# A diffusion-transformer kernel: the last output tile's second half in column parts of 384 and 128, in place of 256 and 256

## The chip, the cores and the metric

One NeuronCore of one Trainium2 chip runs the whole kernel. The metric is the device time of one execution in microseconds. The kernel before took 1170.2 us, the median of three runs that lie between 1170.05 and 1171.52 us. One further execution was recorded by the profiler; every trace number below comes from it.

## What is computed

The reference is a two-layer network on 256 latent tokens and 256 context tokens of width 1024. Each layer has adaptive modulation, a token mixer (retention in the first layer, neighbourhood attention in the second), a gated residual with layer norm, and a squared-ReLU MLP with hidden width 4096. Only the last lines of the second layer matter here:

```python
def sq_relu_mlp(h, w1, w2):
    return jnp.square(jax.nn.relu(h @ w1)) @ w2

x = layer_norm(DN_ALPHA * x + g1 * y, ln_g[i, 0], ln_b[i, 0])
h = x * (1.0 + sc2) + sh2
x = layer_norm(DN_ALPHA * x + g2 * sq_relu_mlp(h, mlp_w1[i], mlp_w2[i]), ln_g[i, 1], ln_b[i, 1])
```

In the last layer only the 256 latent rows go through the MLP, and the last `layer_norm` writes the output.

## The kernel before

Every product of two float32 matrices is made as three products of rounded operands. Each operand is split into a high part in the type float32r and a low part (the value less its high part, again float32r), and `mm3` issues high*high, high*low and low*high into one PSUM accumulator. Each of the three is its own MATMUL with its own weight load (LDWEIGHTS).

The second matrix of the last MLP (4096 x 1024) is streamed from memory in 32 **units** of 256 rows x 512 columns: SyncE issues the load into `raw` (a ring of four buffers), ScalarE makes the high part (`hi`, a CAST), VectorE makes the low part (`lo`). The high and low tiles come from rings of five (`hip`, `lop`); three more homes in freed memory (`spares`) hold units fetched further ahead, and these are called `unit` in the trace. `fetch_ahead` decides which unit goes where.

The hidden activations `hid` are stationary: each weight load brings 128 hidden channels x 128 tokens into the array, and the unit's columns stream past it. The output has two token tiles (t = 0, 1) of 128 rows, and two halves of 512 columns each. Four accumulations, each in PSUM banks of its own, are kept open over the whole of the MLP:

- (0,0), (0,1) and (1,0) each have one bank and one part of 512 columns;
- (1,1), the last tile's second half, has two banks. `parts[1, 1]` lists the columns of each.

The loop `for step in range(24)` takes one unit at a time (u = step // 2, half = step % 2) and calls `mm2b(t, half, u, un)` for both tiles. `mm2b` runs over the parts of that accumulation, and for each part issues 2 x 3 = 6 MATMULs. So the split of (1,1) is used in **every** odd step, not at the end alone: in each of the 12 odd steps part 0 gets six MATMULs and then part 1 gets six.

The last eight units are held (`held`), and the tail uses them accumulation by accumulation, so that the accumulations end one after the other: (0,0), (0,1), (1,0), then part 0 of (1,1) in 24 MATMULs, then part 1 of (1,1) in 24 MATMULs. Behind each, VectorE multiplies the product by the gate `G2`, adds it to the residual `R`, and takes the row statistics (`bn_stats`). For the second token tile this goes by four pieces, called quarters: `gate_quarter`, `add_quarter` and `stat_quarter` for q = 0 to 3. `moments` joins the four statistics, GpSimd makes the reciprocal standard deviation, and `finish_last` makes the two passes of the layer norm and starts the last three stores (512, 256 and 256 columns).

The order of the instructions on each engine is written by hand from the tail on (`e.on = True`). Before that, in the 24 steps, PE, ScalarE, VectorE and GpSimd are ordered by the scheduler of the tile framework, which works from its own estimate of times; SyncE is always in program order, apart from where that estimate places an instruction.

Of the kernel before, what the change touches and what calls it, by code (L numbers as in the profile page):

```python
# [93 lines left out]
def kernel(  # L94
# [23 lines left out]
    pe, act, dve, pool, sp = (  # L118
        InOrder(tc, getattr(nc, e), e in PIN)
        for e in ("tensor", "scalar", "vector", "gpsimd", "sync")  # L120
    )
# [19 lines left out]
    def nm(s):  # L141
        uid[0] += 1
        return f"{s}_{uid[0]}"

    def bank(s="ps"):
        return psp.tile([P, 512], F32, tag="ps", name=nm(s))
# [5 lines left out]
    def scr(s, dt=F32):  # L152
        return scp.tile([P, 512], dt, tag="scr", name=nm(s))
# [201 lines left out]
    R = [RR[t // 2][:, t % 2, :] for t in range(4)]  # L355
# [232 lines left out]
    def load_gate(l, w, nt=2, eng=nc.scalar):  # L588
        G = cpool.tile([P, 2, D], F32, tag="G", name=nm("G"))
        gt = grow[l, w]  # L590
        for t in range(nt):
            eng.dma_start(out=G[:, t, :], in_=gt[t : t + 1, :].broadcast_to([P, D]))
        return G
# [486 lines left out]
    for h in range(RH):  # L1080
# [105 lines left out]
        for t in range(4):  # L1186
            po = bank("po")
            scs = list(range(4)) if t < 2 else [2, 3]
            for i, sc in enumerate(scs):
# [9 lines left out]
                out=on, in0=po[:], scalar1=mv[:, 0:1], scalar2=r[:], op0=ALU.subtract, op1=ALU.mult  # L1199
# [47 lines left out]
        else:  # L1247
# [17 lines left out]
            def turn(t):  # L1265
                return [mod_pt(xns[t], half) for half in range(2)]
# [75 lines left out]
    G2 = None  # L1342
    for hf in range(2):
# [9 lines left out]
        if hf == 0:  # L1353
# [6 lines left out]
            p2 = turn(2)  # L1360
# [45 lines left out]
        for half in range(2):  # L1406
# [14 lines left out]
            for u in range(8 - nheld):  # L1421
# [4 lines left out]
                if G2 is None and bg_done[0] >= 36:  # L1426
                    G2 = load_gate(0, 1)
# [21 lines left out]
            def settle(t):  # L1449

                add_to(t, 1, gated(pb[t], t, 1, G2), dve)
                stat(t, 1)
                return moments(t)
# [13 lines left out]
            m = settle(0)  # L1467
# [5 lines left out]
            m = settle(1)  # L1473
# [9 lines left out]
            m = settle(2)  # L1483
# [328 lines left out]
    m = settle(3)  # L1812
# [3 lines left out]
    p2 = turn(2)  # L1816
# [144 lines left out]
    def wo_last(ps, t, half, cols=slice(0, 512), first=False):  # L1961
        mmo(ps, t, (4, 5, 6, 7), us[half::2], cols, first)
        return ps
# [13 lines left out]
    ps = wo_last(bank("pnw"), 0, 0, first=True)  # L1977
# [61 lines left out]
    ps = [bank("pnw") for _ in range(2)]  # L2039
# [63 lines left out]

    FULL = slice(0, 512)
    parts = {(t, half): [(bank("p2"), FULL)] for t, half in ((0, 0), (0, 1), (1, 0))}
    parts[1, 1] = [(bank("p2"), slice(256 * q, 256 * q + 256)) for q in range(2)]

    def mm2b(t, half, u, un, only=None):
        wh, wl = un
# [32 lines left out]
    for step in range(24):  # L2142
# [7 lines left out]
        if step == 11:  # L2150
            bg_until(83)
            G2 = load_gate(1, 1, 1)
# [6 lines left out]
        e.on = True  # L2159
    st1 = scr("st1")[:, :24].rearrange("p (q s) -> p q s", q=4)  # L2160

    def quarter(q):
        return slice(256 * q, 256 * q + 256)

    gq = {}

    def gate_quarter(q):
        ps = parts[1, q // 2][(q // 2) * (q % 2)][0][:, quarter(q % 2)]
        gq[q] = scr("acc")
        dve.tensor_mul(out=gq[q][:, :256], in0=ps, in1=G2[:, 0, quarter(q)])  # L2170

    def add_quarter(q):
        dve.tensor_add(out=R[1][:, quarter(q)], in0=R[1][:, quarter(q)], in1=gq[q][:, :256])

    def stat_quarter(q):
        dve.bn_stats(out=st1[:, q, :], in_=R[1][:, quarter(q)])
# [3 lines left out]
    def store(t, sl, q=sp):  # L2180
        q.dma_start(out=by_grid(out[0], t)[:, :, sl], in_=xn2[:, t, sl])

    def last_norm(t, a, sl, mv, r, q=sp):

        xn = xn2[:, t, sl]
        dve.scalar_tensor_tensor(
            out=xn,
            in0=xn if a else R[t][:, sl],
            scalar=r[:] if a else mv[:, 0:1],
            in1=gb[:, a, sl],  # L2190
            op0=ALU.mult if a else ALU.subtract,
            op1=ALU.add if a else ALU.mult,
        )
        if a:
            store(t, sl, q)
# [8 lines left out]
    def finish_last(m):  # L2204
        for half in range(2):
            last_norm(1, 0, HALF[half], *m)
        last_norm(1, 1, HALF[0], *m)
        for q, queue in ((2, act), (3, sp)):
            last_norm(1, 1, quarter(q), *m, queue)

    for half in range(2):
        for u in range(12, 16):
# [10 lines left out]
    for q in range(4):  # L2223
        gate_quarter(q)
        add_quarter(q)
        stat_quarter(q)
    stats[1] = st1
    finish_last(moments(1))


# [29 lines left out]
```

## Time and profile before

| what | before |
|---|---|
| median of the runs | 1170.2 us |
| lowest and highest run | 1170.05, 1171.52 us |
| the profiled execution, whole time | 1170.31 us |
| its span, first to last instruction | 1168.4 us |
| granted TensorE clock, mean | 0.998 |
| DVE, ACT, POOL busy | 67%, 45%, 14% of the span |
| first matmul of the last product | 1071.30 us |
| last matmul of it begins | 1159.96 us |
| VectorE's last instruction begins | 1164.42 us, 0.48 us long |

All trace times are microseconds from the span's start; the profiled execution is 1.9 us longer than its span. In the views, PE is the matmul side of TensorE and PEld its weight loads, DVE is VectorE, ACT is ScalarE, POOL is GpSimd, SP is SyncE, and a q behind a name is the engine's own queue. A row of the timeline gives start, length, engine, line, operation, output<-inputs, the tile of the array in rows*columns (for PE), the operand's shape, and xN where N instructions alike were merged into one row, from the first start to the last end. Almost all rows have line 84, which is the helper that records every operation, so tiles are told apart by their names: `p` is a product in PSUM, `hi`, `lo` and `unit` are weights, `hid` the hidden activations. In the PE rows the type of float32r operands is printed as f32.

In the trace matmuls overlap: those of 256 columns are printed as 0.28 us long and start 0.12 us apart. What a stream of matmuls costs is read from the distance between starts.

### The profile page before, as it was taken

What the parts mean: (1) busy time and instruction counts of PE and PEld (TensorE: products, weight loads), DVE (VectorE), ACT (ScalarE), POOL (GpSimd) and SP (SyncE); (2) the same over time, 40 slices, a digit from 0 to 9 for tenths busy, and PEclk for the clock granted to TensorE, in tenths of its full rate; (3) what the DMA queues carried; (4) which work ended last, traced back from release to release, by engine and by line L of the source; (5) the groups of instructions that cost most, each with busy time, mean ns of one, the idle gap of its engine ahead of it and who ended that gap; (6) DMA issues with size and microseconds to landing.
All of it is one profiled execution on the core that took longest, in us unless ns stands there. A gap on an engine that the chain in (4) does not pass through costs nothing.

```text
span 1168.4 us, 18111 instructions
## 1 busy us (share of the span) xinstructions
PE 1154.2 (99%) x7114; PEld 977.5 (84%) x7114; DVE 779.5 (67%) x1223; ACT 520.6 (45%) x900; POOL 157.9 (14%) x187
## 2 busy tenths in 40 slices
PE   9999999999999999999999999999999999999997
PEld 6788888888888889888888788889777879999886
DVE  3585797689597476368877666658456578865555
ACT  3643342243323247442123553127466685776350
POOL 0102002100200150000202000221253450000000
PEclk9999999999999999999999999999999999999999
DMA  9742552856345224357665667635634453686860
GB/s 322 236 130 87 162 166 78 297 154 213 98 148 185 78 59 120 87 146 247 203 198 166 213 200 249 201 108 184 200 112 154 143 187 109 203 252 225 272 221 36
DMA packets 134470, 200.06 MB, mean 171 GB/s; under 512 B 16193, under 2 KB 76385, under 8 KB 134385
## 3 DMA queue, kind: packets, MB, share of 16 engines
q1 hardware_dynamic: 129696, 185.69, 50.2%
q0 software_dynamic: 3296, 10.55, 2.9%
q10 hardware_dynamic: 1392, 2.67, 0.7%
q8 instruction: 56, 0.92, 0.3%
q14 instruction: 30, 0.24, 0.1%
HBM read 190.36 MB, written 10.61 MB: 172 GB/s over the span
## 4 chain that ended last, share of the span: by engine, by line
PE 82%; DVE 6%; DMA 6%; ACT 3%; issue 2%; POOL 1%; DVEq 0%; POOLq 0%; ACTq 0%; SPq 0%
PE p L84 34%; PE pw L84 7%; PE pv L84 7%; PE pq L84 7%; PE pg L84 7%; PE pnv L84 4%; PE pn L84 3%; PE po L84 3%; DVE acc L84 2%; DMA rawa<-in_ada_w_dram 2%; PE pnw L84 2%; DMA raw<-in_mlp_w_dram 2%; PE pS L84 1%; DVE lo L84 1%; PE pt L84 1%
## 5 line engine op out<-in xcount | busy, mean ns | idle before, releaser
L84 ACT CAST hi<-raw 128x1024 fp32r<-128x1024 f32 (+1 forms) x222 | 222.4, 1012 | 323.5 <-DMA raw<-in_mlp_w_dram 115.4
L84 DVE TENSOR_TENSOR lo<-raw,hi 128x1024 fp32r<-128x1024 f32 (+1 forms) x210 | 249.6, 1200 | 131.5 <-ACT hi L84 129.5
L84 PE MATMUL p<-hi,hid 128*128 128x512 f32 (+1 forms) x792 | 230.7, 373 | 0.0
L84 PE MATMUL p<-hTh,hi 128*128 128x256 f32 (+1 forms) x512 | 168.5, 330 | 0.0
L84 PE MATMUL p<-hTh,lo 128*128 128x256 f32 (+1 forms) x512 | 168.0, 329 | 0.0
L84 PEld LDWEIGHTS p<-hi,hid 128*128 128x128 f32 x792 | 145.0, 188 | 26.0
L84 PE MATMUL p<-hTl,hi 128*128 128x256 f32 (+1 forms) x512 | 166.2, 329 | 0.0
L84 PE MATMUL p<-lo,hid 128*128 128x512 f32 (+1 forms) x396 | 147.4, 372 | 0.0
L84 PEld LDWEIGHTS p<-hTh,lo 128*128 128x128 f32 x512 | 97.3, 190 | 8.8
L84 PEld LDWEIGHTS p<-hTh,hi 128*128 128x128 f32 x512 | 97.3, 190 | 8.7
L84 PEld LDWEIGHTS p<-hTl,hi 128*128 128x128 f32 x512 | 96.3, 190 | 8.6
L84 DVE SCALAR_TENSOR_TENSOR acc<-rawa,scol,acc 128x1024 f32<-128x1024 f32 x63 | 80.8, 1309 | 21.5 <-DMA rawa<-in_ada_w_dram 21.2
L84 PEld LDWEIGHTS p<-lo,hid 128*128 128x128 f32 x396 | 74.6, 188 | 12.8
L84 DVE SCALAR_TENSOR_TENSOR strips<-rawa,scol,strips 128x512 f32<-128x512 f32 x84 | 57.5, 744 | 0.0
L84 DVE TENSOR_TENSOR hid<-r,hid 128x512 fp32r<-128x512 f32 (+1 forms) x60 | 33.5, 571 | 30.6 <-ACT hid L84 30.6
L84 ACT ACTIVATE r<-p 128x512 f32<-128x512 f32 (+1 forms) x60 | 29.7, 496 | 52.2 <-PE p L84 52.1
L84 POOL DMA_DIRECT2D grow<-grow x6 | 3.3, 557 | 366.5 <-DVE grow L84 366.5
L84 PE MATMUL pw<-hi,oh 128*128 128x512 f32 x128 | 50.8, 397 | 0.0
L84 PE MATMUL pg<-hi,hTh 128*128 128x512 f32 x128 | 50.6, 396 | 0.0
L84 PE MATMUL pv<-hi,hTh 128*128 128x512 f32 x128 | 50.4, 394 | 0.0
L84 PE MATMUL pw<-hi,ol 128*128 128x512 f32 x128 | 49.9, 390 | 0.0
L84 PE MATMUL pg<-hi,hTl 128*128 128x512 f32 x128 | 49.9, 390 | 0.0
(235 smaller groups left out, 2251.9 us busy)
## 6 DMA issues: line engine op xcount, KB each, us to landing
raw<-in_mlp_w_dram SPq DMA_DIRECT2D x128, 512.0 KB
rawa<-in_ada_w_dram SPq DMA_DIRECT2D x80, 512.0 KB
raw<-in_ret_w_in_dram SPq DMA_DIRECT2D x46, 512.0 KB
raw<-in_nat_w_in_dram SPq DMA_DIRECT2D x24, 512.0 KB
rawq<-in_ada_w_dram SPq DMA_DIRECT2D x16, 512.0 KB
raw<-in_ret_w_o_dram SPq DMA_DIRECT2D x16, 512.0 KB
rpb_near<-far SPq DMA_DIRECT2D x20, 256.0 KB
bias<-rpb_near POOLq DMA_DIRECT2D x16, 320.0 KB, 4.6
```

The costliest lines, as they stand in the source:

```text
L84: r = f(*args, **kwargs)
```

## The change

`parts[1, 1]` gets the columns 0 to 383 and 384 to 511 of the half, in place of two parts of 256. The gate, the sum and the statistics of the second token tile follow: the first two pieces stay at 256 columns, the third has 384 and the fourth 128. The stores and the two passes of the layer norm keep their columns.

```diff
-    parts[1, 1] = [(bank("p2"), slice(256 * q, 256 * q + 256)) for q in range(2)]
+    LATE = [slice(0, 384), slice(384, 512)]
+    parts[1, 1] = [(bank("p2"), cols) for cols in LATE]
...
+    QUARTERS = [slice(0, 256), slice(256, 512)] + [slice(512 + s.start, 512 + s.stop) for s in LATE]
+    gq = {}
+
     def quarter(q):
-        return slice(256 * q, 256 * q + 256)
-
-    gq = {}
+        return QUARTERS[q]
 
     def gate_quarter(q):
-        ps = parts[1, q // 2][(q // 2) * (q % 2)][0][:, quarter(q % 2)]
-        gq[q] = scr("acc")
-        dve.tensor_mul(out=gq[q][:, :256], in0=ps, in1=G2[:, 0, quarter(q)])
+        ps = parts[1, q // 2][(q // 2) * (q % 2)][0][:, LATE[q - 2] if q > 1 else quarter(q)]
+        gq[q] = scr("acc")[:, : ps.shape[1]]
+        dve.tensor_mul(out=gq[q], in0=ps, in1=G2[:, 0, quarter(q)])
 
     def add_quarter(q):
-        dve.tensor_add(out=R[1][:, quarter(q)], in0=R[1][:, quarter(q)], in1=gq[q][:, :256])
+        dve.tensor_add(out=R[1][:, quarter(q)], in0=R[1][:, quarter(q)], in1=gq[q])
...
-        for q, queue in ((2, act), (3, sp)):
-            last_norm(1, 1, quarter(q), *m, queue)
+        for q, queue in ((0, act), (1, sp)):
+            last_norm(1, 1, slice(512 + 256 * q, 768 + 256 * q), *m, queue)
```

On PE, in the first odd step of the loop, the two parts of (1,1) stand like this before; `p_1630` is the bank of part 0, `p_1631` that of part 1, and `hi` and `lo` are the unit's two tiles:

```order
L84 MATMUL p_1630_10459<-hi_10383,hid_1435_9144 128x256
L84 MATMUL p_1630_10459<-lo_10384,hid_1435_9144 128x256
L84 MATMUL p_1630_10459<-hi_10383,hid_1435_9144 128x256 x2
L84 MATMUL p_1630_10459<-lo_10384,hid_1435_9144 128x256
L84 MATMUL p_1630_10459<-hi_10383,hid_1435_9144 128x256
L84 MATMUL p_1631_10460<-hi_10383,hid_1435_9144 128x256
L84 MATMUL p_1631_10460<-lo_10384,hid_1435_9144 128x256
L84 MATMUL p_1631_10460<-hi_10383,hid_1435_9144 128x256 x2
L84 MATMUL p_1631_10460<-lo_10384,hid_1435_9144 128x256
L84 MATMUL p_1631_10460<-hi_10383,hid_1435_9144 128x256
```

In the change the same twelve matmuls stand in the same order:

```order
L84 MATMUL p_1630_10459<-hi_10383,hid_1435_9144 128x384
L84 MATMUL p_1630_10459<-lo_10384,hid_1435_9144 128x384
L84 MATMUL p_1630_10459<-hi_10383,hid_1435_9144 128x384 x2
L84 MATMUL p_1630_10459<-lo_10384,hid_1435_9144 128x384
L84 MATMUL p_1630_10459<-hi_10383,hid_1435_9144 128x384
L84 MATMUL p_1631_10460<-hi_10383,hid_1435_9144 128x128
L84 MATMUL p_1631_10460<-lo_10384,hid_1435_9144 128x128
L84 MATMUL p_1631_10460<-hi_10383,hid_1435_9144 128x128 x2
L84 MATMUL p_1631_10460<-lo_10384,hid_1435_9144 128x128
L84 MATMUL p_1631_10460<-hi_10383,hid_1435_9144 128x128
```

Nothing moved there: the number of matmuls and of weight loads is the same, six are 384 columns wide and six are 128. The same is true of the other 11 odd steps, and of the 24 and 24 matmuls of the tail.

On ScalarE, about half-way through the loop, the scheduler puts three casts in another order; `hi` tiles are in the ring of five, `unit` tiles in the spare homes, and the numbers of `raw` rise in the order in which PE uses the units:

```order
 L84 CAST hi_10777<-raw_10775 128x1024
 L592 DMA G_10728<-grow_107 128x1024
+L84 CAST unit_10807<-raw_10805 128x1024
 L84 CAST hi_10783<-raw_10781 128x1024
-L84 CAST unit_10807<-raw_10805 128x1024
 L84 CAST hi_10801<-raw_10799 128x1024
+L84 CAST unit_10836<-raw_10834 128x1024
 L84 CAST hi_10830<-raw_10828 128x1024
-L84 CAST unit_10836<-raw_10834 128x1024
+L84 CAST unit_10859<-raw_10857 128x1024
 L84 CAST hi_10853<-raw_10851 128x1024
-L84 CAST unit_10859<-raw_10857 128x1024
```

Each of three `unit` casts now stands one cast earlier, ahead of a `hi` cast whose weights PE uses sooner. VectorE's subtractions move in the same way.

On SyncE one load moves: the second row of layer-norm constants now goes out ahead of a weight unit instead of behind it:

```order
 L84 DMA raw_10638<-in_mlp_w_dram 128x2x512
 L84 DMA gb_10772<-in_ln_g_dram 128x1024
+L84 DMA gb_10772<-in_ln_b_dram 128x1024
 L84 DMA raw_10656<-in_mlp_w_dram 128x2x512
-L84 DMA gb_10772<-in_ln_b_dram 128x1024
 L84 DMA raw_10680<-in_mlp_w_dram 128x2x512
```

So one weight unit of the loop, `raw_10656`, now stands one load later in SyncE's queue. No other instruction changes its place.

## The prediction

> **What bounds the kernel now.** I read the page first, then the chain that ended last, then the groups of matmuls of the last product, then the timeline around the rows that these pointed to.
>
> ```profile
> span 1168.4 us, 18111 instructions
> PE 1154.2 (99%) x7114; PEld 977.5 (84%) x7114; DVE 779.5 (67%) x1223; ACT 520.6 (45%) x900; POOL 157.9 (14%) x187
> PEclk9999999999999999999999999999999999999999
> ```
>
> PE is busy all the time at the full clock. The chain says how the end is reached (start, length, what):
>
> ```profile
> 996.58 108.11 PE p L84 x804
> 1104.70 0.14 PE pada L84 x2
> 1104.84 55.42 PE p L84 x300
> 1160.26 0.02 issue
> 1160.28 0.44 DVE acc L84
> ...
> 1161.20 0.44 DVE st L84
> ...
> 1164.50 0.40 DVE xn L84
> ```
>
> From 996 us on the chain is nothing but matmuls, until 1160.26. Then VectorE's gate (`acc`), sum (`R`) and statistics (`st`) of the last 256 columns stand on it one by one, then the norm. So each nanosecond by which a matmul of the last product follows later is paid in full, and what shortens those three VectorE steps is gained in full. The groups by form in the stretch of that product (xN | busy us, mean ns | idle before):
>
> ```profile
> L84 PE MATMUL p<-hi,hid 128*128 128x256 f32 x128 | 25.1, 282 | 0.0
> L84 PE MATMUL p<-lo,hid 128*128 128x256 f32 x64 | 18.1, 283 | 0.0
> ```
>
> 128 + 64 = 192 matmuls of 256 columns: all belong to the accumulation that the change re-cuts. The words "last tile" mislead: 96 matmuls become 384 wide and 96 become 128 wide, spread over all 16 row pairs of the product, and PE never idles before one.
>
> **What a matmul of each width costs.** The measure is the distance between starts. Six matmuls of 512 columns lie between these two rows, and ten of 256 between the next two:
>
> ```profile
> 1150.25 0.39 PE L84 MATMUL p<-hi,hid 128*128 128x512 f32 x1
> ...
> 1151.61 0.39 PE L84 MATMUL p<-unit,hid 128*128 128x512 f32 x1
> ```
>
> ```profile
> 1158.76 0.28 PE L84 MATMUL p<-lo,hid 128*128 128x256 f32 x1
> ...
> 1159.96 0.28 PE L84 MATMUL p<-hi,hid 128*128 128x256 f32 x1
> ```
>
> 1.36 / 6 = 0.2267 us, and 1.20 / 10 = 0.120 us. The line through both is 0.0133 us plus 0.417 ns a column. It gives 0.1733 us at 384 columns, which lies between the two measured widths, so I take it. At 128 columns it gives 0.0667 us; then a pair would cost 0.240, as two of 256 do now, and PE would lose nothing. The question is whether 128 columns are long enough to cover the next weight load, since every matmul here has its own. Three rows answer. First, four matmuls of only 4 columns with full weights:
>
> ```profile
> 35.30 0.52 PEld L84 LDWEIGHTS pada<-cst,row 128*128 128x128 f32 x4 [0.20 <-DVE row L84]
> ```
>
> ```profile
> L84 PEld LDWEIGHTS pada<-cst,row x16: 186/190/192, 11.6 to 47.6; 128*128 128x128 f32 x16
> ```
>
> A load is 0.19 long, so four follow each other at (0.52 - 0.19) / 3 = 0.11 us, though the columns would need 0.015 by the line. Second, the scores of the attention, the only float32r matmuls under 256 columns: 160 wide, in rounds of four (one on each quarter of the array's rows). The timeline cut after two rounds, and after three:
>
> ```profile
> 815.21 0.46 PE L84 MATMUL pqk<-kT,qT 32*128 32x160 f32 x8
> ```
>
> ```profile
> 815.21 0.57 PE L84 MATMUL pqk<-kT,qT 32*128 32x160 f32 x12
> ```
>
> A round adds 0.11 us; the line would give 0.080. Third, transposes of exactly this tile, 128 columns:
>
> ```profile
> 990.01 0.60 PE L84 MATMUL pt<-cst,r 128*128 128x128 f32 x4
> L84 PE MATMUL pt<-cst,r 128*128 128x128 f32 x8 | 1.4, 273 | 0.0
> ```
>
> (0.60 - 0.273) / 3 = 0.109 us. I take **0.11 us** for a matmul of 128 columns, paced by the weight load of the next. The bounds are 0.067 (the line, nothing lost to loads) and 0.120 (the measured 256 columns).
>
> The Trainium skill's page "TensorE: Matmul & The Clock Gate", section "Back-to-back issue gap", speaks against this: for streams of weight load and matmul pairs it gives about 81 ns a matmul at 128 columns. By it the sum below would be +1.0 us, not +3.7. The same sentence gives 131 ns at 512 columns, where this trace has 227, so I do not lean on it.
>
> **The sum.** Four terms, in us:
>
> 1. 96 matmuls at 0.1733 in place of 0.120: +5.12.
> 2. 95 distances behind the narrow ones (the very last has none) at 0.11 in place of 0.120: -0.95. The narrow matmuls come in blocks of six, and 24 at the end, so a load has no wide neighbour to hide under but for the first of a block.
> 3. The very last matmul streams 128 columns fewer before VectorE can start: -0.05 (128 x 0.417 ns).
> 4. VectorE's last three steps at 128 columns:
>
> ```profile
> 1149.09 0.69 DVE L84 TENSOR_TENSOR acc<-p,G 128x512 f32<-128x512 f32 x1 [3.29 <-PE p L84]
> ...
> 1150.54 0.69 DVE L84 BATCH_NORM_STATS2 st<-R 128x6 f32<-128x512 f32 x1
> ```
>
> ```profile
> 1160.28 0.42 DVE L84 TENSOR_TENSOR acc<-p,G 128x256 f32<-128x256 f32 x1 [1.53 <-PE p L84]
> 1160.74 0.42 DVE L84 TENSOR_TENSOR R<-R,acc 128x256 f32<-128x256 f32 x1
> 1161.20 0.43 DVE L84 BATCH_NORM_STATS2 st<-R 128x6 f32<-128x256 f32 x1
> ```
>
> ```profile
> L84 DVE TENSOR_TENSOR rt<-pav,rt x16: 271/290/297, 851.2 to 967.7; 128x128 f32<-128x128 f32 x16
> ```
>
> 0.69 at 512 and 0.42 at 256 make 0.285 at 128 by the line, and the one operation of that width that the trace has is 0.290. Three steps save 0.13 each: -0.39. For statistics at 128 no row exists; between no gain and the whole 0.43 I take the line.
>
> Together 5.12 - 0.95 - 0.05 - 0.39 = **+3.7 us**. The profiled execution took 1170.31 us in all, so 1174.0; the median of the runs, 1170.2, is 0.1 lower.
>
> What is hidden: the gate, sum and statistics of the 384 columns cost 0.555 each by the same line, with 0.035 between them 1.74 us, and part 1's matmuls last 24 x 0.11 = 2.64 us; if that cover fell short, the rest would be added. Now it is shown to be ample: VectorE waited 1.53 us for PE before the last gate.
>
> The reordered casts cost nothing while the weights stay ahead. These are, before the change, the cast of the unit of step 18 and the spare unit that now goes first, and then the first matmul of the product:
>
> ```profile
> 1110.48 1.05 ACT L84 CAST hi<-raw 128x1024 fp32r<-128x1024 f32 x1 [1.74 <-PE p L84]
> 1112.23 1.05 ACT L84 CAST unit<-raw 128x1024 fp32r<-128x1024 f32 x1 [0.69 <-DMA raw<-in_mlp_w_dram]
> ```
>
> ```profile
> 1071.30 0.40 PE L84 MATMUL p<-hi,hid 128*128 128x512 f32 x1
> ```
>
> The spare's cast waits for its own load until 1112.23. Put first, it makes the other wait in ScalarE's strict order until 1113.28, 2.8 us later than now. The later loads, whose `raw` buffers come free behind that subtraction, slip by about as much. Two steps cost 18 x 0.2267 + 12 x 0.120 = 5.52 us, so step 18 begins near 1071.3 + 9 x 5.52 = 1121. Cast and subtraction of its unit would end near 1115.6: 5 us to spare, and PE comes 2 us later than now. The layer-norm row that goes ahead of a weight load on SyncE is one load of 0.5 MB; the unit behind it belongs to step 12, near 1104.4:
>
> ```profile
> 1086.92 0.37 SPq L84 DMA_DIRECT2D raw<-in_mlp_w_dram  x1
> ```
>
> That is 17 us ahead. All of this I cost at nothing; if the cover were gone, up to 3 us would come on top.
>
> **The rivals.**
>
> *A, the forecast: weight loads pace the narrow matmuls.* From 0.108 to 0.120 a matmul: +3.5 to +4.7, so 1173.8 to 1175.0. Chance 0.82.
>
> *B, not slower: the next load is pulled far enough ahead, and 128 columns run at the line's 0.067.* Then term 2 is -5.04 and the sum is -0.36: 1169.9. For it speaks that 64-row loads of the transposes in the attention go closer:
>
> ```profile
> 828.22 0.76 PEld L84 LDWEIGHTS ppt<-cst,s 64*128 64x128 f32 x22 [0.35 <-issue]
> ```
>
> These are 22 loads in pairs, 0.14 long each: (0.76 - 0.14) / 10 = 0.06 a pair. Against it: they use half of the array's rows, and all three rows at full tiles or in float32r say 0.11. It decides at a pace of 0.071 us, where the sum is zero; the sum exceeds 0.2% (2.3 us) only above 0.095. The page's 81 ns, above, falls in this case too. Chance 0.10.
>
> *C, dearer columns: float32r under 256 columns falls to the rate of plain float32.* The trace has plain float32 at 128 and 64 columns:
>
> ```profile
> L84 PE MATMUL pav<-pt,natv 128*32 128x128 f32 x128 | 6.6, 279 | 0.0
> L84 PE MATMUL pav<-pt,natv 128*32 128x64 f32 x64 | 2.4, 219 | 0.0
> ```
>
> 60 ns for 64 columns is about twice the line's rate, and each such product is recorded twice, so four times: 0.0133 + 128 x 1.67 ns = 0.227 us. Then term 2 is +10.2 and the time 1185.1. The 160-wide rounds, at 0.11 and not 0.28, speak against it. Chance 0.04.
>
> *D, weights late: the slips above add up and PE waits in the loop.* 1 to 3 us on top of A, 1175 to 1177. Chance 0.04. That the change does not do what it says is ruled out by the built order.
>
> **How the numbers follow.** A is the likeliest: 1174.0. The range 1172.8 to 1175.8 takes in A with both ends of its pace (0.100 as the low end, which gives +2.8, less 0.2 for the spread of the runs; 0.120 as the high end, plus 0.8 for VectorE's unshown steps, that spread and the near part of D); B and C, 0.14 together, stay out, since they lie far off. What a measurement of this kernel can tell from no change is about 0.2%, 2.3 us. Slower by more than that: A, C, D, 0.90. Within it: B, 0.09. Faster: 0.01, only B with all of VectorE's gain and more.
>
> **What would show it.** The timeline of the changed kernel's last matmuls should show 24 of 128 columns about 0.11 apart, and weight loads back to back; those of 384 columns 0.173 apart. The last product should take 4.2 us more, VectorE's tail from the last matmul to `mv` 0.4 less, and PE's idle time in the product stay 0. Narrow matmuls 0.07 apart would prove B, 0.22 apart C, and a wait of PE for `hi`, `lo` or `unit` D.

## The result and the profile after

| what | before | after |
|---|---|---|
| median of the runs | 1170.22 us | 1176.58 us |
| lowest and highest run | 1169.75, 1171.91 us | 1175.54, 1177.42 us |
| the profiled execution, whole time | 1170.31 us | 1175.54 us |
| span | 1168.4 us | 1173.8 us |
| granted TensorE clock, mean | 0.998 | 0.998 |

The changed kernel is slower: the ratio is 1.0052, with a 95% interval of 1.0040 to 1.0064. The forecast was 1174.0 us with a range up to 1175.8. The direction came out as forecast, and the measured median lies 0.8 us above the range. The profiled execution is the fastest of the six runs, so the profile shows a smaller difference than the medians, 5.2 us.

The chain of waits of the changed kernel (start, length, what), in the stretch that the prediction showed of before:

```profile
997.35 110.00 PE p L84 x804
1107.34 0.19 PE pada L84 x2
1107.54 58.46 PE p L84 x300
1166.00 0.02 issue
1166.02 0.30 DVE acc L84
...
1166.67 0.30 DVE st L84
...
1169.83 0.40 DVE xn L84
```

The chain has the same form as before. Its three pieces of PE work add up to 110.00 + 0.19 + 58.46 = 168.65 us. Before they were 108.11 + 0.14 + 55.42 = 163.67, so the product takes **4.98 us more**. From the end of PE's work to the start of the last norm it is 1169.83 - 1166.00 = 3.83 us, and before it was 4.24: **0.41 us less**. The difference that the cut itself makes is thus +4.57 us. What is left in this one profile is that the product starts later: its first matmul begins at 1072.06 us instead of 1071.30.

Where that 0.76 comes from can be followed upstream. It is there before the product begins, in the attention: in the waits between 850 and 880 us, VectorE's wait for a DMA is 2.0 us in the profile of before, and in that of the changed kernel it is this (us in total, times, longest):

```profile
DVE s L84 <- DMA bias<-rpb_near: 2.7, 1, 2.7
```

This load is a piece of the chain that ended last, here before and then after the change (start, length, what):

```profile
857.39 5.17 DMA bias<-rpb_near
```

```profile
857.50 5.86 DMA bias<-rpb_near
```

It took 0.69 us longer and began 0.11 later. The change touches nothing there. The repeated executions below show that this start wanders in both directions.

The matmuls in the stretch of the last product, grouped by form (xN | busy us, mean ns | idle before):

```profile
L84 PE MATMUL p<-hi,hid 128*128 128x384 f32 x64 | 18.6, 339 | 0.0
...
L84 PE MATMUL p<-hi,hid 128*128 128x128 f32 x64 | 12.1, 263 | 0.0
...
L84 PE MATMUL p<-lo,hid 128*128 128x384 f32 x32 | 10.8, 337 | 0.0
L84 PE MATMUL p<-lo,hid 128*128 128x128 f32 x32 | 8.8, 275 | 0.0
```

The four rows add up to 96 matmuls of 384 columns and 96 of 128, as forecast, and PE idles ahead of none of them. A matmul with a third of the columns is printed nearly as long as the wide one, 263 to 275 ns against 337 to 339. The lengths overlap, so the distance between starts decides. The timeline of the changed kernel's last matmuls:

```profile
1162.32 0.33 PE L84 MATMUL p<-lo,hid 128*128 128x384 f32 x1
...
1162.84 0.33 PE L84 MATMUL p<-lo,hid 128*128 128x384 f32 x1
...
1163.58 0.28 PE L84 MATMUL p<-lo,hid 128*128 128x128 f32 x1
...
1165.59 0.28 PE L84 MATMUL p<-lo,hid 128*128 128x128 f32 x1
1165.71 0.28 PE L84 MATMUL p<-hi,hid 128*128 128x128 f32 x1
```

There are three matmuls from the first row to the second: 0.52 / 3 = 0.173 us at 384 columns. From the third row to the fourth there are 18 of 128 columns: 2.01 / 18 = 0.112 us. Both are the forecast prices. Inside the loop it looks different. One odd step there, in the same view:

```profile
1088.07 0.34 PE L84 MATMUL p<-lo,hid 128*128 128x384 f32 x1
...
1088.61 0.34 PE L84 MATMUL p<-lo,hid 128*128 128x384 f32 x1
1088.78 0.40 PE L84 MATMUL p<-hi,hid 128*128 128x384 f32 x2
1089.02 0.27 PE L84 MATMUL p<-lo,hid 128*128 128x128 f32 x1
...
1089.47 0.56 PE L84 MATMUL p<-hi,hid 128*128 128x128 f32 x2
1089.87 0.40 PE L84 MATMUL p<-lo,hid 128*128 128x512 f32 x1
```

Three of 384 columns take 0.54 here (1088.07 to 1088.61), 0.18 each and not 0.173. The row at 1089.47 holds two matmuls, the last of 128 columns and the first of 512 behind it. Together they take 0.40 us until 1089.87, where 0.11 + 0.227 = 0.34 was to be expected. So matmuls behind a change of width come later than their price, and that is where the product lost what the forecast did not have.

The cycle of two steps, worked out start by start from the trace (ns from each matmul's start to the next, medians over the cycles of the loop):

```
before   18 of 512:  234 235 229 232 231 227, then 226 or 227
         12 of 256:  113 119 120 120 120 120 120 120 120 120 120 120    cycle 5540
after    18 of 512:  285 235 233 236 224 231 236 228 232 231, then 227
          6 of 384:  171 175 178 185 176 182
          6 of 128:   60 111 112 111 113 110                           cycle 5867
```

Nine of the loop's twelve cycles repeat this within 2 ns. The changed kernel's first cycle has no narrow block ahead of it and is shorter (5789), and in both kernels the two cycles beside the two `pada` matmuls are longer. In the tail the first six matmuls of 384 columns show the same distances (171, 175, 177, 185, 176, 182), and those behind them settle at 173 to 174.

VectorE's last steps in the changed kernel (the brackets give the wait ahead of an instruction):

```profile
1163.39 0.56 DVE L84 TENSOR_TENSOR acc<-p,G 128x384 f32<-128x384 f32 x1 [1.59 <-PE p L84]
...
1164.57 0.56 DVE L84 BATCH_NORM_STATS2 st<-R 128x6 f32<-128x384 f32 x1
1166.02 0.29 DVE L84 TENSOR_TENSOR acc<-p,G 128x128 f32<-128x128 f32 x1 [0.89 <-PE p L84]
1166.34 0.29 DVE L84 TENSOR_TENSOR R<-R,acc 128x128 f32<-128x128 f32 x1
1166.67 0.29 DVE L84 BATCH_NORM_STATS2 st<-R 128x6 f32<-128x128 f32 x1
```

The three steps on 384 columns are hidden, with 0.89 us to spare, and the three on 128 take 0.29 each, the statistics too.

### The profile page after: what moved, and what is told of

It reads as the page before. It is cut to its first block, busy times and chain, and to the rows that moved or that the text cites. A ratio compares the mean times of both kernels' runs of the same rounds, so it can differ in the third digit from the quotient of the medians.

```text
span 1173.8 us, 18111 instructions
## 1 busy us (share of the span) xinstructions
PE 1158.8 (99%) x7114; PEld 981.6 (84%) x7114; DVE 780.9 (67%) x1223; ACT 520.5 (44%) x900; POOL 159.3 (14%) x187
## 4 chain that ended last, share of the span: by engine, by line
PE 82%; DVE 6%; DMA 6%; ACT 3%; issue 2%; POOL 1%; ACTq 0%; DVEq 0%; POOLq 0%; SPq 0%
PE p L84 34%; PE pw L84 7%; PE pv L84 7%; PE pg L84 7%; PE pq L84 7%; PE pn L84 4%; PE pnv L84 4%; PE po L84 3%; DMA raw<-in_mlp_w_dram 2%; DVE acc L84 2%; PE pnw L84 2%; DMA rawa<-in_ada_w_dram 2%; DVE lo L84 1%; PE pS L84 1%; ACT hi L84 1%
## 5 line engine op out<-in xcount | busy, mean ns | idle before, releaser
L84 PE MATMUL p<-hi,hid 128*128 128x512 f32 (+2 forms) x792 | 235.0, 377 | 0.0
L84 PE MATMUL p<-lo,hid 128*128 128x512 f32 (+2 forms) x396 | 148.8, 376 | 0.0
```

The costliest lines, as they stand in the source:

```text
L84: r = f(*args, **kwargs)
```

## The experiments

Three questions were open: where the 0.81 us come from by which the product exceeded its forecast (4.98 against 4.17), whether the rest of the excess belongs to the change, and whether the weight load really sets the pace of the narrow matmuls. In what follows "product" is the time from the first to the last start of a matmul of the last product, and "VectorE's tail" is the time from there to the end of VectorE's last instruction; "the tail" alone stays the kernel's last eight units:

| kernel | start of the product | product | VectorE's tail |
|---|---|---|---|
| before | 1071.30 | 88.67 | 4.93 |
| before_again | 1070.43 | 88.67 | 4.93 |
| after | 1072.06 | 93.65 | 4.52 |
| after_again | 1071.01 | 93.65 | 4.53 |
| after_third | 1070.28 | 93.65 | 4.53 |
| narrow_first | 1071.21 | 93.51 | 4.53 |
| split_320 | 1070.08 | 90.49 | 4.73 |
| split_448 | 1071.20 | 95.96 | 4.33 |
| half_rows | 1071.79 | 88.93 | 4.68 |
| half_rows_both | 1072.44 | 88.95 | 4.68 |
| alternate | 1071.35 | 93.21 | 4.53 |
| fresh_256 | 1071.81 | 87.51 | 4.93 |
| fresh_384 | 1071.79 | 88.58 | 4.53 |

**The same kernels again** (before_again, after_again, after_third; no edit).

> The kernel before once more, timed against itself, to see what of the result is chance. The product of the last MLP (first to last matmul start) should last 88.66 us again, to a few hundredths. Theory 'chance upstream': the first matmul of that product starts anywhere from 1070.5 to 1072.5 us, as it moved from 1071.30 to 1072.06 between the two profiles on record, and the ratio to the kernel before has an interval some 0.1% wide on each side of 1. Theory 'the change acts upstream': this kernel starts the product at 1071.3 within 0.3 us every time.

> The changed kernel once more. Product 93.65 us again, end of VectorE 4.5 us after the last matmul start. Theory 'chance upstream': the difference to the kernel before, +6.3 us in the first measurement, falls towards the +4.6 us that product and tail account for (+4.0 to +5.5), and the start of the product lies within 1 us of that of before_again. Theory 'the change acts upstream': +6 us or more again, and a start of the product at 1072 us or later.

> The changed kernel a third time, because the first two measurements gave +6.4 and +4.8 us. Theory 'chance upstream' (the true effect is what product and tail show, +4.6 us): a difference to the kernel before of +4 to +5.5 us, product 93.65 us. Theory 'the first measurement was the true one': +6 us or more.

before_again came out at 1.0004 (0.9995 to 1.0013) of before. The changed kernel came out at 1.0040 (1.0027 to 1.0054; 1174.77 against 1169.93 us, +4.84) and then at 1.0029 (1.0019 to 1.0038; 1175.05 against 1171.09 us, +3.96). The chain of after_third:

```profile
995.57 110.00 PE p L84 x804
1105.57 0.20 PE pada L84 x2
1105.76 58.46 PE p L84 x300
```

The lengths 110.00 and 58.46 are those of after, while the start lies 1.78 us earlier. Product and VectorE's tail repeat to about 0.01 us. The start of the product wanders between 1070.1 and 1072.4 over all the profiled executions, of whichever kernel. So 4.57 us, 0.39%, is the constant part of the change, and the middle one of the three ratios is nearly that. The 1.8 us on top in the first measurement is in no trace's product or VectorE's tail, and it did not repeat. The intervals of the first and the third comparison do not overlap.

One thing did differ in the runs that have no trace: the mean granted clock, which the record lists for most runs. The profiled run of the first measurement had 0.998, the other five 0.996 to 0.997. Over the listed runs of these two kernels, those at 0.996 have medians of 1172.9 us (before, 4 runs) and 1176.6 (after, 5 runs), and those at 0.998 have 1170.5 (33 runs) and 1174.8 (10 runs). So the excess goes with a lower granted clock. Which of the two brings about the other is not shown: in the two traces of the first measurement the clock is at 0.50 only behind the last matmul (from 1164.0 us on before, from 1168.4 after), and no run at 0.996 has a trace.

**narrow_first**: in the loop the part of 128 columns goes ahead of that of 384; the tail stays.

```diff
-        for i, (ps, cols) in enumerate(parts[t, half]):
+        for i, (ps, cols) in list(enumerate(parts[t, half]))[:: -1 if only is None else 1]:
```

> As the changed kernel, but in the 12 odd steps of the loop the six matmuls of 128 columns stand ahead of the six of 384; the tail is unchanged. Theory 'load floor alone' (0.111 us a narrow matmul, 0.1733 for 384, 0.2267 for 512, order of no account): two steps last 5.79 us in either order, where 5.867 was measured for the first order. Theory 'a change of width costs time by itself' (some 27 ns spread over the next matmuls, seen after 512 to 384 and after 256 to 512): still three changes in two steps, so again 5.84 to 5.90 us, with the slow matmuls now behind the change from 128 to 384 and from 384 to 512.

The cycle took 5.853 us, the product 93.51, the one execution 1174.56. The distances were 58, 112, 113, 110, 111, 115 for the narrow ones, then 225, 168, 177, 185, 176, 182 for those of 384, then slow ones of 512 again. A cycle of the plain prices 0.11, 0.173 and 0.227, 5.79 us in either order, is refuted. The one large distance (225 in place of 171) follows the narrow block to where it now stands, and the uneven rhythm stands behind both changes to a wider part.

**split_320**: the columns at 320 and 192.

```diff
-    LATE = [slice(0, 384), slice(384, 512)]
+    LATE = [slice(0, 320), slice(320, 512)]
```

> Parts of 320 and 192 columns in place of 384 and 128, in the loop, the tail, the gate, the sum and the statistics. Theory 'load floor': 192 columns (0.093 us by the line) are still under the floor, so their starts are 0.111 us apart as with 128, and 320 columns 0.147: a pair 0.258 against 0.285 with 384 and 128 and 0.240 before; the product lasts 96 x 0.018 = 1.7 us more than before, 90.4, and with 0.06 us a loop step for changes of width 91.1. Theory 'narrow matmuls cost more a column': 192 columns cost visibly more than 128, over 0.12 us. Theory 'columns alone': 0.093 us, and the product lasts 88.7 us.

The timeline of split_320's last matmuls:

```profile
1158.78 0.27 PE L84 MATMUL p<-lo,hid 128*128 128x192 f32 x1
...
1160.45 0.28 PE L84 MATMUL p<-lo,hid 128*128 128x192 f32 x1
```

15 matmuls lie between these rows: 1.67 / 15 = 0.111 us at 192 columns, where the line of the columns gives 0.0133 + 192 x 0.417 ns = 0.093. 192 columns cost as much as 128. In the loop the six of 320 columns are not slow (143 to 147 ns; the line gives 147), though they too stand behind a change of width. The product takes 90.49, 1.82 more than before. The one execution took 1170.62, with a product that happened to start early, at 1070.08.

**split_448**: the columns at 448 and 64, by the same line.

> Parts of 448 and 64 columns in place of 384 and 128. Theory 'the weight load paces': 64 columns (0.040 us by the line) cost 0.111 us again, and 448 cost 0.200, so a pair costs 0.311 and the product lasts 96 x 0.071 = 6.8 us more than before, 95.5 us, up to 96.5 with what the changes of width cost; the last matmul start to the end of VectorE falls to 4.3 us. Theory 'a cost by columns': a pair 0.240, product 88.7 us.

```profile
1165.71 0.28 PE L84 MATMUL p<-lo,hid 128*128 128x64 f32 x1
...
1167.05 0.28 PE L84 MATMUL p<-lo,hid 128*128 128x64 f32 x1
```

There are 12 matmuls from row to row: 1.34 / 12 = 0.112 us at 64 columns. From 192 to 64 the columns fall to a third and the distance does not move. The product takes 95.96, the one execution 1176.82.

**half_rows**: this takes the suspected cost away. The narrow part is computed for the first 64 of the tile's 128 token rows only, so that its weight loads have 64 columns. The other 64 rows of that part stay zero: this kernel leaves them out.

```diff
+    dve.memset(parts[1, 1][1][0][:, 384:], 0.0)
...
+                    rows = 64 if i else P
-                        ps[:, cols],
-                        (ht[:, k % 4, 0, tsl(t)], ht[:, k % 4, 1, tsl(t)]),
+                        ps[:rows, cols],
+                        (ht[:, k % 4, 0, t * P : t * P + rows], ht[:, k % 4, 1, t * P : t * P + rows]),
```

> As the changed kernel, but the part of 128 columns is computed for 64 of its 128 token rows only (the other 64 stay zero): each of its 96 weight loads brings 64 columns in place of 128, while the matmuls stream 128 columns as before. Theory 'the weight load paces the narrow matmuls': a load of half the columns takes about 0.055 us, so starts fall to the line's 0.067 us, and the product from 93.65 to about 89.4 us (95 x 0.0446 less) or a little under. Theory 'a fixed cost per matmul' (issue, or the stream itself): 0.111 us as before, product 93.65 us.

The timeline of half_rows, its matmuls and then its weight loads, and last the loads at the same place of the changed kernel:

```profile
1159.76 0.22 PE L84 MATMUL p<-lo,hid 128*64 128x128 f32 x1
...
1160.66 0.22 PE L84 MATMUL p<-lo,hid 128*64 128x128 f32 x1
```

```profile
1160.12 0.20 PEld L84 LDWEIGHTS p<-hi,hid 128*64 128x64 f32 x2
1160.24 0.14 PEld L84 LDWEIGHTS p<-lo,hid 128*64 128x64 f32 x1
```

```profile
1165.31 0.30 PEld L84 LDWEIGHTS p<-hi,hid 128*128 128x128 f32 x2
1165.53 0.19 PEld L84 LDWEIGHTS p<-lo,hid 128*128 128x128 f32 x1
```

15 matmuls take 0.90: 0.060 us each, still with 128 columns streamed. From the first of two loads to the one behind them it is 0.12 / 2 = 0.06 us, and 0.22 / 2 = 0.11 in the changed kernel. So with half the load's columns the pace fell from 0.111 to 0.060, and the product is 88.93: of the 4.98 us only 0.26 are left. A load of 64 columns also makes a product of 64 rows, and this run cannot part the two. For the load speak the distances of the loads themselves, the same 0.11 us at 64, 128 and 192 streamed columns, and the four-column matmuls with full loads that the prediction read, 0.11 us too. VectorE's tail is 0.15 longer than after's, since 24 x 0.060 = 1.44 us no longer cover VectorE's 1.74 us of work on 384 columns.

**half_rows_both**: both parts of (1,1) for 64 rows only (`rows = 64 if (t, half) == (1, 1) else P`), so that no load of that block is long. The other 64 rows of (1,1) stay zero.

> As the run with 64 of 128 token rows in the part of 128 columns, but the part of 384 columns is computed for 64 rows too (the other 64 of the last tile's second half stay zero), so all 192 weight loads of these parts bring 64 columns. What is open is why the first six matmuls of 384 columns behind another width start 0.178 us apart and not 0.173, and why up to ten of 512 columns behind narrow ones are slow. Theory 'the load's length': the six of 384 come at 0.173 (1.040 us in place of 1.066), and the block of 512 behind the narrow ones is no longer than in the run with the narrow part halved (18 in 4.151 us). Theory 'the width alone': 1.059 to 1.066 us again.

The six of 384 columns took 1.042 us a cycle instead of 1.066, so their slowness goes with the length of the loads among them. Yet the 18 of 512 columns behind the narrow ones took 4.173 us, with a first distance of 282; they take 4.151 in half_rows, 4.185 in the changed kernel and 4.107 in the kernel before. Most of their slowness stayed, though the loads ahead of it were short. The length of the loads alone does not explain it.

**alternate**: in the loop the matmuls of 384 and 128 columns take turns, so that every narrow one has a wide neighbour on both sides.

```diff
+        if only is None and len(parts[t, half]) > 1:
+            for kk in range(2):
...
+                for j, (lhs, w) in enumerate(((hh, wh), (hh, wl), (hl, wh))):
+                    for ps, cols in parts[t, half]:
+                        pe.matmul(ps[:, cols], lhsT=lhs, rhs=w[:, kk, cols], start=k == 0 and j == 0, stop=k == 31 and j == 2)
+            return
```

> As the changed kernel, but in the odd steps of the loop a matmul of 384 columns and one of 128 take turns, in place of six and six; the tail is unchanged. Theory 'load floor, one load ahead': a pair costs 0.173 + 0.111 = 0.285 as before, two steps 5.79 us, or 5.87 with what the changes of width cost in blocks. Theory 'a change of width costs 27 ns each time': 11 changes more, two steps about 6.1 us. Theory 'loads can run further ahead': the wide matmul covers the load behind the narrow one, a pair costs 0.240, two steps 5.52 us.

One loop step of alternate (a row holds the matmuls of both widths):

```profile
1087.34 0.45 PE L84 MATMUL p<-lo,hid 128*128 128x384 f32 x2
1087.62 0.74 PE L84 MATMUL p<-hi,hid 128*128 128x384 f32 x4
1088.19 0.45 PE L84 MATMUL p<-lo,hid 128*128 128x384 f32 x2
```

Three pairs take 0.85, 0.285 a pair: 58 ns behind the narrow one's start and 228 behind the wide one's. That is 0.173 + 0.111 = 0.284 again, the plain sum, so a wide neighbour hides none of the narrow one's load. The cycle is 5.827. Of the three theories one load ahead (5.79 to 5.87) fits. Loads that run further ahead (5.52) missed, and so did a price of 27 ns on every change of width (6.1), which had been the second explanation of the slow matmuls.

**fresh_256** and **fresh_384**: in the loop (1,1) has one bank and one part of 512 columns. The tail's eight units go into two fresh banks, at 256 and 256 or at 384 and 128, and VectorE adds the loop's bank to the residual while PE works on the tail.

```diff
-    LATE = [slice(0, 384), slice(384, 512)]
-    parts[1, 1] = [(bank("p2"), cols) for cols in LATE]
+    LATE = [slice(0, 256), slice(256, 512)]
+    loop_bank = bank("p2")
+    parts[1, 1] = [(loop_bank, FULL)]
+    ends = {}
...
-                        k == 0, k == 31,
+                        k == ends.get((t, half), 0), k == (23 if (t, half) == (1, 1) and not ends else 31),
...
+    add_to(1, 1, gated(loop_bank, 1, 1, G2), dve)
+    parts[1, 1] = [(bank("p2"), cols) for cols in LATE]
+    ends[1, 1] = 24
```

(fresh_384 keeps the first line as the change has it.)

> The last tile's second half is multiplied in the loop as one part of 512 columns, so no width changes there; the tail's eight units go into two fresh banks of 256 columns each, and VectorE adds the loop's bank to the residual while PE works on the first accumulation of the tail. Computes the reference. Theory 'load floor alone': two steps of the loop last 24 x 0.2267 = 5.44 us against 5.52 by the line with 256, so 12 x 0.08 = 1.0 us less than the kernel before. Theory 'changes of width cost too': against the measured 5.540, so 12 x 0.10 = 1.2 us less, and no slow matmuls anywhere in the loop after the first five. Both: product 87.4 to 87.7 us, VectorE's tail unchanged at 4.93, the run about 1169 us, hardly to be told from the kernel before by its time. If VectorE's two extra steps of 0.69 us stand in the way, the end comes up to 1.4 us later.

> The change in the tail alone: the loop as in the run with fresh banks (one part of 512 columns), the tail in parts of 384 and 128 with gate, sum and statistics by them. Against that run with 256 and 256 in the tail (product 87.51 us, tail 4.93): the 24 wide matmuls cost 24 x 0.053 = 1.28 us more, the 23 distances behind narrow ones 0.2 us less, so product 88.58 us and tail 4.52; together 0.66 us later. Rival 'the cut pays where it was meant to': a product under 87.9 us, so that the 0.41 us of VectorE wins.

fresh_256's chain, and then its VectorE around the added sum:

```profile
997.10 107.55 PE p L84 x768
1104.65 0.14 PE pada L84 x2
1104.79 54.82 PE p L84 x264
```

```profile
1139.80 0.68 DVE L84 TENSOR_TENSOR acc<-p,G 128x512 f32<-128x512 f32 x1
1140.51 0.69 DVE L84 TENSOR_TENSOR R<-R,acc 128x512 f32<-128x512 f32 x1
1143.01 0.69 DVE L84 TENSOR_TENSOR acc<-p,G 128x512 f32<-128x512 f32 x1 [1.80 <-PE p L84]
```

107.55 + 0.14 + 54.82 = 162.51, that is 1.16 less than before. The two added steps on VectorE end 1.8 us ahead of the next product and cost nothing. The ratio to before is 0.9986 (0.9977 to 0.9996; 1170.17 against 1171.09 us). It is clearly faster than the changed kernel, 1175.05 in the same series. Against before the interval leaves out 1 by little, and two such intervals above did not overlap though they measured the same pair; what is sure is the 1.16 us of the product. fresh_384's piece is 55.88 in place of 54.82, so its product is 1.06 longer, and its VectorE's tail is 0.40 shorter. 384 and 128 columns thus lose 0.66 us even where the cut acts in the tail alone. Its one execution took 1170.21.

## Why the prediction was right or wrong

**The mechanism (A) held.** The prediction took 0.11 us for 128 columns, "paced by the weight load of the next". 64, 128 and 192 columns all come 0.111 to 0.112 apart. When the load was halved and the streamed columns were not, the distance fell to 0.060, a little under the line's 0.067. B (0.067) and C (0.227) are out.

On the load itself, the Trainium skill's page "TensorE: Matmul & The Clock Gate", section "LDWEIGHTS (loading the stationary operand)", gives the columns of the load divided by 1.2 as its ns; an estimate worked out from that is 107 for 128 columns and 53 for 64. The measured paces of 111 and 60 lie 4 and 7 ns above it. The Trainium skill's 81 ns, from the section "Back-to-back issue gap" of the same page, spoke against the forecast; the 111 ns measured at 128 columns do not agree with it.

**D fell.** PE idles before no matmul of the product, so the casts and the weight load that moved were hidden, as forecast.

**Terms 3 and 4** were -0.05 and -0.39, together -0.44, counted up to VectorE's steps. VectorE's tail shrank by 0.41. The statistics at 128 columns, the one step that no row had shown, took 0.29 as by the line, and the three steps on 384 columns stayed hidden.

**Terms 1 and 2 failed in size, in the loop.** They gave +5.12 and -0.95, net +4.17; the product grew by 4.98. The tail's 48 matmuls came out as forecast (+1.07 against +1.05). The loop's twelve cycles cost 0.327 us more each, against 0.260:

| a cycle's part | by the prediction | measured | missed, us |
|---|---|---|---|
| six of 384 columns | 6 x 0.1733 = 1.040 | 1.066 | 0.026 |
| six of 128, with the 0.058 that they push onto the first of 512 behind them | 6 x 0.11 = 0.660 | 0.674 | 0.014 |
| the other 512s behind them | as before | slower | 0.020 |
| twelve of 256, before | 12 x 0.120 = 1.440 | 1.433 | 0.007 |

These make 0.067 a cycle and 12 x 0.067 = 0.80 us, which is the 0.81 by which the forecast of the product was short. The sum took one price a width, whatever stands ahead. The prices of 256 and 512 columns had been read in the tail, that of 384 from the line through them, and that of 128 from short streams elsewhere; in the tail's runs of 24 they come out. In the loop (1,1) never has more than six alike, and there the matmuls behind a change of width come later. That this slowness exists, and where, the traces show. Its cause is only partly settled: it is not a fixed price on a change of width (alternate), and matmuls of 320 columns are free of it (split_320). Shorter loads remove it at 384 columns, but at the 512s behind only a part of it (half_rows, half_rows_both).

**The spread of the runs** is the other step that failed, in "How the numbers follow". The high end of the range took in "0.8 for VectorE's unshown steps, that spread and the near part of D", and the low end 0.2 for the spread, though the same section puts at 2.3 us what a measurement can tell from no change. With the measured 4.57 the profiled execution of before gives 1170.31 + 4.57 = 1174.9, inside the range. The first measurement lies 1.7 us higher still, in runs that go with a lower granted clock. The start of the product alone wanders over 2.4 us, and runs of the unchanged kernel lie between 1168.4 and 1175.9. The three runs before the change, within 1.5 us of each other, hid that. The later comparisons, 1174.77 and 1175.05, fell inside the range.

## What to carry to other kernels

Before making the moving side of a matmul narrower, find what one weight load costs in that stream (here 0.111 us for 128 stationary columns, as much as some 235 columns by the line): below that width the columns saved are not gained. A cut meant for the end of an accumulation acts in every step if the accumulation is open all along, so give the end banks of its own, and the loop keeps its widest shape. Take a matmul's price from a run of the same length and neighbours as the place where it will stand, and the uncertainty of a small effect from more than a handful of runs.

## What the runs showed of the hardware

Behind a change of moving width, matmuls of 384 and of 512 columns keep a fixed uneven rhythm, those of 512 for about ten matmuls (285, 235, 233, 236, 224, 231, 236, 228, 232, 231 ns, then 227), the same within 2 ns in nine of the twelve cycles. The first narrow matmul of a block has the next only 0.060 us behind it, and the first wide one behind the block has the next 0.285 behind it in place of 0.227. The two distances make up for each other: 30 + 314 ns at 64 columns (split_448), 60 + 285 at 128 and 88 + 257 at 192 (split_320), 344 or 345 each time. Why is not shown; with half the load the two are 60 and 285 again (half_rows). And a wide neighbour hides none of a narrow matmul's load: taking turns costs the plain sum, 0.285 us a pair.
